# A matmul with RMS norm on one core: block 4's scaled copy in gamma's space, two norms ahead of the evictions, and the head's transposes three matmuls later

## The chip, the cores and the metric

The kernel runs on one core of one Trainium2 chip. The metric is the device time of one execution in microseconds (us). Profile times count from the start of the profiled span, which is 1.8 us shorter than the device time of the same run.

## The reference

```python
def reference(a, b, gamma, eps):          # a, b: 2048 x 2048 float32, gamma: 2048
    x = np.matmul(a, b)
    rms = np.sqrt(np.mean(x ** 2, axis=-1, keepdims=True) + eps)
    return (gamma * x / rms).astype(np.float32)
```

## The kernel before

The output has 16 blocks of 128 rows. Matmuls write into *banks* of the memory called PSUM; copying a finished bank out, by ScalarE or VectorE, is called *evicting* it. A *K tile* is 128 steps of the dimension that is summed over. Blocks 0 to 3 are the "head": while a and b stream in, chunk by chunk, TensorE transposes a's chunk (in a *pair* of K tiles, `kp` = 0 to 7) and multiplies at once. From the right half of blocks 2 and 3 on, and for all later pairs of blocks, the kernel uses Strassen's scheme: seven products ("product 1" to "product 7") of quarter blocks, from sums of quarters that VectorE prepares. Blocks from 4 on are first scaled by a power of two to fp16 (`row_norm`, `row_factor`, `row_apply`), then transposed.

In the code below, `x11` to `x22` are the quarters of one pair's output, `P` is 128, `HB` is 4 (the first block after the head), and left-out lines are marked `...`. Four places matter. First, one PSUM bank, `tbank`, serves both the head's transposes and the one output chunk of the head that finds no bank of its own (`stream_in_parts`):

```python
ps_t = ctx.enter_context(tc.tile_pool(name="ps_t", bufs=1, space=bass.MemoryType.PSUM))

def transpose_head(kp):
    bank = ps_t.tile([P, CH], FP32, name="tbank")
    ...                                            # 8 transposes of 128x128 into it
    nc.vector.tensor_copy(out=head_at[:, 2 * kp:2 * kp + 2, :, :], in_=view)

def stream_in_parts(g, kp):
    part = ps_t.tile([P, CH], FP32, name="tbank")
    ...                                            # 2 matmuls into it, then a copy or an add

for kp in range(KP):
    ...
    before = [lambda: transpose_head(kp + 1)] if kp + 1 < KP else []
    ...
    # the pair's 14 matmuls, with the next pair's transposes after the 7th (12th in pair 0)
    stream(groups1, kp, before, len(groups1) + 5 if kp == 0 else None)
    ...
    stream_in_parts(last1, kp)
    ...
```

Second, block 4's scaled copy goes to the third quarter of `head_at`, which product 3 of the head's Strassen pair still reads:

```python
def a16_slot(mb):
    flat = head_at.rearrange("p t r m -> p (t r m)").bitcast(FP16)
    return flat[:, (2 + mb % 2) * K:(3 + mb % 2) * K]
```

Third, what happens between the head and the first later group; the order of these lines is the order on each engine:

```python
nc.gpsimd.dma_start(out=gamma_sb, in_=gamma.partition_broadcast(P))
load_block(HB + 2)                                  # block 6
load_block(HB + 3)                                  # block 7
...
nc.scalar.copy(out=x22, in_=pair[2])
nc.vector.tensor_tensor(out=x22, in0=pair[5], in1=x22, op=ALU.add)
evict(plain, (2, 3))                                # four banks: two ScalarE, two VectorE
b_sums_in_place(1, KP - 1)
product(PAIR, 1, 4, pair[2], start=False)
row_norm(HB)                                        # ScalarE, block 4
row_norm(HB + 1)                                    # ScalarE, block 5
nc.vector.tensor_tensor(out=x22, in0=pair[1], in1=x22, op=ALU.subtract)
row_factor(HB)                                      # VectorE, four small ones
product(PAIR, 1, 3, pair[5], start=False)
row_apply(HB)                                       # VectorE, 128x2048
nc.scalar.copy(out=x21, in_=pair[2])
row_factor(HB + 1)
row_apply(HB + 1)
...
product(PAIR, 1, 7, p7, within={5: [lambda: turn(HB, 0)]})   # transposes of block 4
turn(HB, 1)
...                                                 # ScalarE copies them out, x12 too
product(PAIR, 1, 6, p6)
a_sums(G0, (5,))
...                                                 # transposes of block 5, VectorE copies
take_rms(0)
a_sums(G0, (2, 1))                                  # the sums for products 2 and 1
```

Fourth, gamma's left half is first read when the left half of block 0 is scaled, some microseconds later.

Of the kernel before, what the change touches and what calls it, by code (L numbers as in the profile page):

```python
# [10 lines left out]
FP16 = mybir.dt.float16  # L11
I32 = mybir.dt.int32
ACTF = mybir.ActivationFunctionType
ALU = mybir.AluOpType
# [3 lines left out]
def kernel(  # L18
# [13 lines left out]
    nc = tc.nc  # L32
    P = 128
# [8 lines left out]
    HALF = N // 2  # L42
    HB = 4
# [34 lines left out]
    spare = [spare[:, 0:CH], consts.tile([P, CH], FP32, name="t_first")]  # L78

    def a16_slot(mb):  # L80
        flat = head_at.rearrange("p t r m -> p (t r m)").bitcast(FP16)
        return flat[:, (2 + mb % 2) * K:(3 + mb % 2) * K]

# [6 lines left out]
    for h, queue in enumerate((nc.sync, nc.scalar)):  # L90
        queue.dma_start(out=a0f[:, 2 * h:2 * h + 2, :],
                        in_=a[2 * h * P:(2 * h + 2) * P, 0:W2].rearrange("(r p) k -> p r k", p=P))
# [10 lines left out]
    def load_head(kp):  # L103
        nc.gpsimd.dma_start(  # L104
            out=ah(kp),
            in_=a[0:HB * P, kp * W2:(kp + 1) * W2].rearrange("(r p) k -> p r k", p=P))
        load_b(0, kp)
# [9 lines left out]
    def load_block(mb):  # L117
        a32[mb] = a_pool.tile([P, K], FP32, name="a32")
        nc.gpsimd.dma_start(out=a32[mb], in_=a[mb * P:(mb + 1) * P, :])
# [27 lines left out]
    gamma_sb = consts.tile([P, N], FP32, name="gamma_sb")  # L147
# [13 lines left out]
    def transpose_head(kp):  # L161
        bank = ps_t.tile([P, CH], FP32, name="tbank")
        view = bank.bitcast(BF16).rearrange("p (t r m) -> p t r m", t=2, r=HB)
        for t in range(2):
            for r in range(HB):
                nc.tensor.matmul(  # L166
                    view[:, t, r, :], ah(kp)[:, r, t * P:(t + 1) * P], identity,
                    is_transpose=True,
                    start=(t == 0 and r == 0), stop=(t == 1 and r == HB - 1),
                )  # L170
        nc.vector.tensor_copy(out=head_at[:, 2 * kp:2 * kp + 2, :, :], in_=view)
# [27 lines left out]
    def new_msq(mb):  # L199
        msq[mb] = msq_pool.tile([P, NCH + 1], FP32, name="msq")  # L200
        n_sq[mb] = 0
# [10 lines left out]
    def row_norm(mb):  # L212

        n2 = stat_pool.tile([P, 2], FP32, name="n2")
        for h in range(2):
            junk = sq_pool.tile([P, 2 * CH], BF16, name="sq")
            nc.scalar.activation(out=junk, in_=a32[mb][:, h * HALF:(h + 1) * HALF],  # L217
                                 func=ACTF.Square, scale=2.0 ** -8, accum_out=n2[:, h:h + 1])
        norm[mb] = stat_pool.tile([P, 1], FP32, name="norm")
        nc.scalar.activation(out=norm[mb], in_=n2[:, 0:1], func=ACTF.Sqrt, bias=n2[:, 1:2],  # L220
                             scale=1.0)

    def row_factor(mb):
        s = stat_pool.tile([P, 1], FP32, name="s")
        nc.vector.tensor_scalar_max(out=s, in0=norm.pop(mb), scalar1=1e-18)
        nc.vector.reciprocal(out=s, in_=s)
        nc.vector.tensor_single_scalar(out=s.bitcast(I32), in_=s.bitcast(I32),  # L227
                                       scalar=0x7F800000, op=ALU.bitwise_and)
        new_msq(mb)
        nc.vector.tensor_scalar(out=msq[mb][:, NCH:], in0=s, scalar1=s, scalar2=float(eps),  # L230
                                op0=ALU.mult, op1=ALU.mult)
        factor[mb] = s

    def row_apply(mb):
        a16[mb] = a16_slot(mb)
        if mb < HB + 2:

            nc.vector.tensor_scalar_mul(out=a16[mb], in0=a32.pop(mb), scalar1=factor.pop(mb))  # L238
        else:
            nc.scalar.activation(out=a16[mb], in_=a32.pop(mb), func=ACTF.Copy,  # L240
                                 scale=factor.pop(mb))


    def quarter(g, r, c):
        if g < G0:
            return head_at[:, c::2, 2 * g + r, :]
        return at(2 * g + r)[:, c::2, :]

    def sum_of(g, s):
        return s_sum[s].bitcast(BF16) if g < G0 else s_sum[s]  # L250

    def a_sums(g, which, lo=0, hi=KP):
        a11, a12, a21, a22 = (quarter(g, r, c) for r in range(2) for c in range(2))
        terms = {1: (a11, a22, ALU.add), 2: (a21, a22, ALU.add), 5: (a11, a12, ALU.add),
                 6: (a21, a11, ALU.subtract), 7: (a12, a22, ALU.subtract)}
        for s in which:
            x, y, op = terms[s]
            nc.vector.tensor_tensor(out=sum_of(g, s)[:, lo:hi, :], in0=x[:, lo:hi, :],  # L258
                                    in1=y[:, lo:hi, :], op=op)
# [4 lines left out]
    def b_sums(j, kp):  # L264

        b11, b12, b21, b22 = (b_quarter(j, kp, r, c) for r in range(2) for c in range(2))
        for n, (x, y, op) in enumerate(((b11, b22, ALU.add), (b12, b22, ALU.subtract),
                                        (b21, b11, ALU.subtract))):
            nc.vector.tensor_tensor(out=sums[j][:, n, kp, :], in0=x, in1=y, op=op)  # L269
# [55 lines left out]
    def x_chunk(mb, c):  # L325
        return x_tile(mb, c // 2)[:, (c % 2) * CH:(c % 2 + 1) * CH]
# [50 lines left out]
    def head_matmul(bank, r, c, kt):  # L377
        nc.tensor.matmul(bank, head_at[:, kt, r, :], head_rhs(c, kt),  # L378
                         start=(kt == 0), stop=(kt == KT - 1))

    def new_bank():
        return ps_a.tile([P, CH], FP32, name="acc")
# [3 lines left out]
    def load_later(n):  # L386
        for _ in range(min(n, len(later))):
            kind, which = later.pop(0)
            load_b(1, which) if kind == "b" else load_half(HB + which // 2, which % 2)

    def stream(groups, kp, before=(), when=None):


        order = [(g, kt) for kt in (2 * kp, 2 * kp + 1) for g in groups]
        if kp == KP - 1 or (kp == 0 and not before):
            order.sort(key=lambda x: groups.index(x[0]))
        for n, (g, kt) in enumerate(order):
            if n == (when or len(groups)):
                for work in before:
                    work()  # L400
            if kt == 0:
                banks[g] = new_bank()
            head_matmul(banks[g], *g, kt)
# [13 lines left out]
    def evict(groups, on_vector):  # L417
        for n, g in enumerate(groups):
            copy = nc.vector.tensor_copy if n in on_vector else nc.scalar.copy
            copy(out=x_chunk(*g), in_=banks[g])  # L420

    PAIR = G0 - 1
    groups1 = [(r, c) for r in range(HB) for c in range(2)][:-1]
# [6 lines left out]
    for kp in range(KP):  # L430
        if kp + 4 < KP:
            load_head(kp + 4)
        else:
            load_later(1)
        before = [lambda: transpose_head(kp + 1)] if kp + 1 < KP else []
        if kp in early_sums:
            before.append(lambda: a_sums(PAIR, *early_sums[kp]))
        stream(groups1, kp, before, len(groups1) + 5 if kp == 0 else None)
        if kp == KP - 1:
            evict(groups1, (1, 3, 5))  # L440
        stream_in_parts(last1, kp)
        if kp > 0:
            b_sums(0, kp - 1)
        if 0 < kp < KP - 2:
            b_sums_in_place(0, kp - 1)
# [4 lines left out]
    plain = [(r, c) for r in range(2) for c in (2, 3)]  # L450
    pair = {}
# [28 lines left out]
    for kp in range(KP):  # L480
# [14 lines left out]
            a_sums(PAIR, (5,), 7, KP)  # L495
        if kp in (3, 4):
            a_sums(PAIR, ((7, 6)[kp - 3],))
    nc.gpsimd.dma_start(out=gamma_sb, in_=gamma.partition_broadcast(P))
    load_block(HB + 2)
    load_block(HB + 3)  # L500

    r2, r3 = HB - 2, HB - 1
    for r in range(HB):
# [1 line left out]
    x11, x12, x21, x22 = (x_chunk(r, c) for r in (r2, r3) for c in (2, 3))  # L505
    nc.scalar.copy(out=x22, in_=pair[2])
    nc.vector.tensor_tensor(out=x22, in0=pair[5], in1=x22, op=ALU.add)
    evict(plain, (2, 3))
    b_sums_in_place(1, KP - 1)
    product(PAIR, 1, 4, pair[2], start=False)  # L510
    row_norm(HB)
    row_norm(HB + 1)
    nc.vector.tensor_tensor(out=x22, in0=pair[1], in1=x22, op=ALU.subtract)
    row_factor(HB)
    product(PAIR, 1, 3, pair[5], start=False)
    row_apply(HB)
    nc.scalar.copy(out=x21, in_=pair[2])
    row_factor(HB + 1)
    row_apply(HB + 1)
    p7 = new_bank()  # L520
    turned = {}

    def turn(mb, g):
        turned[mb, g] = transpose_half(mb, g, g == 0)

    product(PAIR, 1, 7, p7, within={5: [lambda: turn(HB, 0)]})
    turn(HB, 1)
    for g in range(2):
        take_transposed(HB, g, turned[HB, g], nc.scalar.copy)
    nc.scalar.copy(out=x12, in_=pair[5])  # L530
    p6 = new_bank()
    product(PAIR, 1, 6, p6)
    a_sums(G0, (5,))
    for g in range(2):
        turn(HB + 1, g)
        take_transposed(HB + 1, g, turned[HB + 1, g], nc.vector.tensor_copy)
# [289 lines left out]
```

## Time and profile before

The kernel before took 222.55 us (median of three, 222.44 to 222.7). The execution that was profiled took 222.79.

| stretch of the profiled run | us |
|---|---|
| start of pair 1 of the head (until then mostly waits for the first chunks) | 11.68 |
| pair 1 to product 4 of the head's Strassen pair | 46.77 |
| product 4 to product 1 of the next group | 12.83 |
| from there to the end | 149.72 |
| span | 221.0 |

The starts are those of matmuls in the timeline of TensorE (PE).

The page's busy times, and its rows of tenths (one digit for each fortieth of the span), for the kernel before:

```profile
PE 210.2 (95%) x1032; PEld 98.1 (44%) x1032; DVE 165.5 (75%) x326; ACT 127.2 (58%) x263; POOL 35.7 (16%) x76
PE   7999999999999999999999999999999999999950
DVE  1218889999989898979695649855794759797690
DMA  7999999999939595947899149945798349044045
```

PE is busy nearly everywhere. The memory system is too, for the first 60 us, and VectorE (DVE) from 16 us on.

The waits of PE, kernel before (engine, line, what it waited for: us in total, times, longest):

```profile
PE acc L145 <- DVE pace L135: 1.5, 1, 1.5
PE tbank L183 <- DVE head_at L238: 0.4, 1, 0.4
PE tbank L409 <- DVE head_at L171: 0.3, 1, 0.3
PE tbank L166 <- DMA early<-in_a_dram: 0.3, 1, 0.3
PE tbank L166 <- DVE t_left L269: 0.2, 1, 0.2
```

L166 is a transpose of the head, L183 one of block 4 or 5, L409 the part in `stream_in_parts`. Apart from the first line, 1.3 us in all (0.40, 0.35, 0.34 and 0.24 in the timeline). The last line names VectorE, but a's chunk, sent at 15.18 and 10.6 us on its way, landed at 25.8, just when that wait ended: both waits of L166 are for chunks of a.

The timeline of PE, kernel before (start, duration, engine, line, operation, output<-inputs, count, idle time before and what ended it):

```profile
13.69 0.62 PE L166 MATMUL tbank<-identity,early 128*128 128x128 bf16 x8 [0.34 <-DMA early<-in_a_dram]
...
25.80 0.62 PE L166 MATMUL tbank<-identity,early 128*128 128x128 bf16 x8 [0.24 <-DVE t_left L269]
...
58.45 3.62 PE L283 MATMUL acc<-early,head_at 128*128 128x512 bf16 x16
...
63.55 0.62 PE L183 MATMUL tbank<-identity_h,head_at 128*128 128x128 f16 x8 [0.40 <-DVE head_at L238]
...
71.28 1.89 PE L283 MATMUL acc<-t_left,s 128*128 128x512 bf16 x8
```

Products 4 and 3 are the 16 matmuls at 58.45; product 1 of the next group starts at 71.28. The three waits are those that the change is after.

ScalarE (ACT) and VectorE before block 4's transposes, timelines of the kernel before:

```profile
57.84 1.08 ACT L420 COPY x<-acc 128x512 f32<-128x512 f32 x2
58.79 1.08 ACT L217 ACTIVATE sq<-a 128x1024 bf16<-128x1024 f32 x1
...
62.21 1.28 DVE L238 TENSOR_SCALAR head_at<-a,s 128x2048 f16<-128x2048 f32 x1
...
66.35 0.69 DVE L258 TENSOR_TENSOR s<-at_even 128x1024 f16<-128x1024 f16 x1 [0.32 <-ACT at_even L190]
```

Two evictions stand ahead of the norm (L217), and the scaled copy (L238) starts at 62.21, 0.3 us after product 3 stops issuing.

The last long piece of the chain that ended last, kernel before:

```profile
67.88 139.98 PE acc L283 x648
```

From 67.88 us on, 648 matmuls follow each other without a gap, at 0.216 us each. What is to be won must be won ahead of that.

### The profile page before, as it was taken

How to read it: one execution, taken by the hardware profiler on the slowest of the kernel's cores; microseconds unless marked ns; L12 is line 12 of the kernel's file. 1: busy time of each engine (PE TensorE's matmuls, PEld its weight loads, DVE VectorE, ACT ScalarE, POOL GpSimd, SP SyncE). 2: the span in 40 equal slices, each digit the busy share in tenths (PEclk: the TensorE clock that was granted, in tenths of full speed). 3: DMA queues.
4: the chain of work that ended last, by engine and by line, in shares of the span. 5: the costliest groups of instructions: out<-in, count | busy, mean ns of one | idle time of the engine just before them, and what ended most of it. 6: DMA issues, size and time to landing. Idle time of an engine off the chain costs nothing.

```text
span 221.0 us, 3043 instructions
## 1 busy us (share of the span) xinstructions
PE 210.2 (95%) x1032; PEld 98.1 (44%) x1032; DVE 165.5 (75%) x326; ACT 127.2 (58%) x263; POOL 35.7 (16%) x76
## 2 busy tenths in 40 slices
PE   7999999999999999999999999999999999999950
PEld 3545445444445444444444444444444444444430
DVE  1218889999989898979695649855794759797690
ACT  2110002920698898688746997299738995334580
POOL 8544343432000002100200002000200000000040
PEclk9999999999999999999999999999999999999995
DMA  7999999999939595947899149945798349044045
GB/s 153 168 203 206 202 206 210 211 208 234 425 113 363 198 296 114 368 174 212 214 303 408 23 88 270 375 202 95 196 288 371 72 89 386 25 190 193 1 191 191
DMA packets 36576, 46.60 MB, mean 211 GB/s; under 512 B 22224, under 2 KB 26320, under 8 KB 35152
## 3 DMA queue, kind: packets, MB, share of 16 engines
q0 software_dynamic: 10464, 23.86, 43.6%
q1 hardware_dynamic: 25680, 22.02, 33.0%
q10 hardware_dynamic: 416, 0.52, 0.7%
q8 instruction: 8, 0.13, 0.2%
q14 instruction: 8, 0.07, 0.1%
HBM read 34.60 MB, written 16.78 MB: 233 GB/s over the span
## 4 chain that ended last, share of the span: by engine, by line
PE 80%; DMA 9%; DVE 5%; POOL 2%; issue 1%; ACT 1%; DVEq 0%; ACTq 0%; POOLq 0%
PE acc L283 67%; PE acc L378 11%; DMA early<-in_a_dram 4%; DMA b<-in_b_dram 4%; POOL b L100 1%; DVE x L704 1%; PE tbank L409 1%; PE tbank L166 1%; POOL early L104 1%; DVE head_at L238 1%; DVE x L707 1%; DVE t_left L269 0%; PE tbank L183 0%; ACT sq L301 0%; PE acc L183 0%
## 5 line engine op out<-in xcount | busy, mean ns | idle before, releaser
L283 PE MATMUL acc<-b,s 128*128 128x512 bf16 x408 | 93.2, 379 | 0.0
L283 PEld LDWEIGHTS <-s 128*128 128x128 f16 (+1 forms) x512 | 49.9, 98 | 59.9 <-DVE s L258 0.4
L378 PE MATMUL acc<-b,head_at 128*128 128x512 bf16 x176 | 43.3, 381 | 0.0
L301 ACT ACTIVATE sq<-x 128x512 bf16<-128x512 f32 x54 | 34.0, 630 | 6.9 <-DVE x L704 3.0
L360 DVE SCALAR_TENSOR_TENSOR x<-x,r,gamma_sb 128x1024 f32<-128x1024 f32 x28 | 34.8, 1282 | 0.7
L217 ACT ACTIVATE sq<-a 128x1024 bf16<-128x1024 f32 x24 | 25.3, 1054 | 2.4 <-DMA a<-in_a_dram 1.9
L378 PEld LDWEIGHTS <-head_at 128*128 128x128 bf16 x176 | 17.0, 99 | 19.3 <-issue 0.7
L240 ACT ACTIVATE head_at<-a,s 128x2048 f16<-128x2048 f32 x10 | 20.0, 1998 | 3.3 <-DVE s L227 3.3
L100 POOL DMA_DIRECT2D b<-in_b_dram x32 | 17.2, 539 | 20.3 <-DMA b<-in_b_dram 14.4
L420 ACT COPY x<-acc 128x512 f32<-128x512 f32 x6 | 3.4, 590 | 25.0 <-PE acc L378 25.0
L283 PEld LDWEIGHTS <-head_at 128*128 128x128 f16 (+1 forms) x112 | 10.9, 98 | 13.2
L283 PE MATMUL acc<-early,head_at 128*128 128x512 bf16 x64 | 14.5, 379 | 0.0
L283 PEld LDWEIGHTS <-at_even 128*128 128x128 f16 x96 | 9.4, 98 | 11.3
L283 PE MATMUL acc<-early,s 128*128 128x512 bf16 x56 | 14.2, 379 | 0.0
L258 DVE TENSOR_TENSOR s<-head_at 128x1024 f16<-128x1024 f16 (+5 forms) x22 | 13.4, 634 | 0.1
L591 DVE TENSOR_TENSOR x<-x,x 128x512 f32<-128x512 f32 x9 | 6.2, 692 | 8.8 <-ACT x L589 8.3
L125 POOL COPY pace<-x 128x1 f32<-128x1 f32 x4 | 1.7, 413 | 66.3 <-DVE x L600 65.1
L573 ACT COPY x<-acc 128x512 f32<-128x512 f32 x9 | 5.2, 573 | 11.5 <-PE acc L283 7.7
L283 PE MATMUL acc<-t_left,s 128*128 128x512 bf16 x48 | 11.3, 379 | 0.0
L274 DVE TENSOR_TENSOR b<-b 128x1024 bf16<-128x1024 bf16 x16 | 10.8, 683 | 0.2
L283 PE MATMUL acc<-t_left,head_at 128*128 128x512 bf16 x48 | 10.9, 379 | 0.0
L283 PE MATMUL acc<-t_left,at_even 128*128 128x512 bf16 x48 | 10.8, 379 | 0.0
(109 smaller groups left out, 223.6 us busy)
## 6 DMA issues: line engine op xcount, KB each, us to landing
out_dram<-x SPq DMA_DIRECT2D x30, 512.0 KB, 3.7
a<-in_a_dram POOLq DMA_DIRECT2D x10, 1024.0 KB, 8.6
b<-in_b_dram POOLq DMA_DIRECT2D x32, 256.0 KB, 9.8
a<-in_a_dram POOLq DMA_DIRECT2D x4, 512.0 KB, 10.0
early<-in_a_dram POOLq DMA_DIRECT2D x7, 256.0 KB, 10.3
gamma_sb<-in_gamma_dram POOLq DMA_DIRECT2D x1, 1024.0 KB, 11.3
out_dram<-a SPq DMA_DIRECT2D x1, 512.0 KB, 3.1
early<-in_a_dram ACTq DMA_DIRECT2D x1, 256.0 KB, 3.5
```

The costliest lines, as they stand in the source:

```text
L100: nc.gpsimd.dma_start(out=raw[j][kp][:, t, :], in_=b[lo:lo + P, j * HALF:(j + 1) * HALF])
L217: nc.scalar.activation(out=junk, in_=a32[mb][:, h * HALF:(h + 1) * HALF], func=ACTF.Square, scale=2.0 ** -8, accum_out=n2[:, h:h + 1])
L240: nc.scalar.activation(out=a16[mb], in_=a32.pop(mb), func=ACTF.Copy, scale=factor.pop(mb))
L258: nc.vector.tensor_tensor(out=sum_of(g, s)[:, lo:hi, :], in0=x[:, lo:hi, :], in1=y[:, lo:hi, :], op=op)
L274: nc.vector.tensor_tensor(out=flat[:, 1:3, :], in0=flat[:, 1:3, :], in1=flat[:, 0::3, :], op=ALU.add)
L283: nc.tensor.matmul(bank, lhsT[:, kp, :], rhs, start=(start and kp == 0), stop=(kp == KP - 1), skip_group_check=not start)
L301: nc.scalar.activation(out=sq[:, 0:CH], in_=src, func=ACTF.Square, scale=inv_sqrt_n, accum_out=msq[mb][:, c:c + 1])
L360: nc.vector.scalar_tensor_tensor(out=x, in0=x, scalar=inverse_of[mb], in1=gamma_sb[:, h * HALF:(h + 1) * HALF], op0=ALU.mult, op1=ALU.mult)
L378: nc.tensor.matmul(bank, head_at[:, kt, r, :], head_rhs(c, kt), start=(kt == 0), stop=(kt == KT - 1))
L420: copy(out=x_chunk(*g), in_=banks[g])
L573: nc.scalar.copy(out=c, in_=one[1])
L591: nc.vector.tensor_tensor(out=t, in0=t, in1=x12, op=ALU.add)
```

## The change

Its intent: take away PE's wait for block 4's copy, by giving the copy a place that nothing else reads and by putting the norms ahead of the evictions; and let a's chunks come later in the head, by asking for their transposes three matmuls later.

```diff
     def a16_slot(mb):
+        if mb == HB:
+            return gamma_sb[:, 0:HALF].bitcast(FP16)
 ...
-        stream(groups1, kp, before, len(groups1) + 5 if kp == 0 else None)
+        stream(groups1, kp, before, len(groups1) + (5 if kp == 0 else 3))
 ...
-    nc.gpsimd.dma_start(out=gamma_sb, in_=gamma.partition_broadcast(P))
+    load_gamma(1)                                   # the right half
     load_block(HB + 2)
-    load_block(HB + 3)
 ...
-    evict(plain, (2, 3))
+    evict(plain[:2], (0, 1))
+    row_norm(HB)
+    row_norm(HB + 1)
+    evict(plain[2:3], ())
+    row_factor(HB)
+    row_apply(HB)
     b_sums_in_place(1, KP - 1)
     product(PAIR, 1, 4, pair[2], start=False)
-    row_norm(HB)
-    row_norm(HB + 1)
-    nc.vector.tensor_tensor(out=x22, in0=pair[1], in1=x22, op=ALU.subtract)
-    row_factor(HB)
     product(PAIR, 1, 3, pair[5], start=False)
-    row_apply(HB)
     nc.scalar.copy(out=x21, in_=pair[2])
     row_factor(HB + 1)
     row_apply(HB + 1)
+    evict(plain[3:], (0,))
 ...
     turn(HB, 1)
+    load_gamma(0)                                   # the left half
+    load_block(HB + 3)
 ...
     a_sums(G0, (5,))
+    nc.vector.tensor_tensor(out=x22, in0=pair[1], in1=x22, op=ALU.subtract)
```

More of the change, by code (lines that the diff above doesn't have):

```diff
@@ L497, with load_gamma @@
             a_sums(PAIR, ((7, 6)[kp - 3],))
-    nc.gpsimd.dma_start(out=gamma_sb, in_=gamma.partition_broadcast(P))
+    def load_gamma(j):
+        half = slice(j * HALF, (j + 1) * HALF)
+        nc.gpsimd.dma_start(out=gamma_sb[:, half], in_=gamma[half].partition_broadcast(P))
+    load_gamma(1)
     load_block(HB + 2)
-    load_block(HB + 3)
     r2, r3 = HB - 2, HB - 1
```

## The prediction

> What bounds the kernel now. The page gives PE 210.2 of 221.0 us busy; the chain of waits is 80% PE, and from 67.88 to 207.86 us it is one unbroken piece of 648 matmuls at 0.216 us each (139.98 us). The waits of PE after its start add up to little: 0.40 us at the first fp16 transpose of block 4 (63.15 to 63.55, for VectorE's scaled copy), 0.35 us for the first head copy, 0.34 us (13.69) and 0.24 us (25.80) before head transposes. So at most about 1 us can be won.
>
> Why block 4 waits. Its scaled copy is written into a quarter of head_at that the product-3 matmuls still read until 61.9; in the timeline VectorE starts it at 62.21 and ends at 63.50. ScalarE evicts two banks (1.08 us) before the norm of block 4 starts at 58.79. In gamma's space the copy has nothing to wait for but the norm. The norm can start near 57.9, its second half when the data lands (48.78 + 10.0 = 58.8); it is ready near 60.3, the factor (0.7 us) and the 1.28 us copy end near 62.3, 0.8 us before PE asks. The 0.40 us goes.
>
> What is added: one VectorE eviction more (0.6 us) and one ScalarE eviction fewer; the x22 subtraction (0.69 us) moves behind block 4's sum, ahead of the sum for product 2 of the next group. Before, that sum (s) ended near 69.45 and the list of waits shows weight loads waiting 0.42 us for it. After: ScalarE's two transposed copies end near 65.7 instead of 66.3; then a sum, the subtraction, two copies, a total, and the sum for product 2: about 69.0. PE without the stall would ask at 69.05 (earlier if the head gains). So about 0.45 us in total passes this point.
>
> Head transposes three matmuls (0.65 us) later: the DMA landings of a's head chunks (13.65, 17.5, 21.35, 25.8, 29.6, 33.4: issue plus landing time) sit within 0.25 us of PE's requests, so both stalls, 0.58 us, go. The copy to head_at (0.69 us) still has about 1.3 us before the next pair. But then b's chunk for the last pair (lands near 35.9, used at 36.2) allows only 0.3 us. That too meets the sum above.
>
> Gamma's left half and block 7. The load waits for the transposes of block 4 (near 64.5), behind block 6, which now goes out near 63.2 (64.40 before). The Trainium skill, "DMA: Bandwidth & Descriptors", section "Anatomy of one DMA — SWDGE (gpsimd) path", fits 2.0 us + bytes/436e3; for 1 MB that is 4.4 us, and block 6 took 5.0 in this trace. By that (an estimate), the 0.5 MB half lands near 70 and is first used near 73.1 (73.52 before). Block 7 goes out near 65.7 (66.58 before) with 0.5 MB more ahead (1.2 us), lands near 73, as before (66.58 + 6.8 = 73.4), and is wanted at 75.3. No new stall expected.
>
> Predicted: 222.55 - 0.45 = 222.1 us, 8 in 10 between 221.5 and 222.6. Faster by over 2%: 0.01; within 2%: 0.97; slower by over 2%: 0.02.
>
> Right if: the wait of PE for the scaled copy is gone; the waits before head transposes are gone or 0.1 us; weight loads of product 2 still wait for s, PE by 0 to 0.4 us; the unbroken piece starts near 67.4 and the span is near 220.5. Wrong if: VectorE waits at the left-half scaling for gamma (a gap near 73), ScalarE for block 7, or PE for banks evicted later or for head copies at the pairs' starts.

## The result, and the profile after

The changed kernel took 222.24 us (median of six, 222.05 to 222.82) against 222.59 us (222.44 to 222.74) for the kernel before. The ratio is 0.9988, with a 95% interval from 0.9975 to 1.0000. A ratio here is the mean time of one kernel's runs over that of the other's of the same rounds, so it is not quite the ratio of the medians.

The gain in time is thus at the edge of the noise. The profiled execution was the slowest of the six (222.82 us), as that of the kernel before was slow for its kind (222.79), so the two spans are alike. Its page and PE waits, changed kernel:

```profile
PE 210.3 (95%) x1032; PEld 98.2 (44%) x1032; DVE 166.6 (75%) x327; ACT 126.7 (57%) x262; POOL 36.2 (16%) x77
```

```profile
PE acc L147 <- DVE pace L137: 1.5, 1, 1.5
PE acc L380 <- DMA b<-in_b_dram: 0.7, 1, 0.7
PE tbank L411 <- DVE head_at L173: 0.4, 1, 0.4
```

The waits at the transposes (now L168 and L185) are gone. A wait for b's first chunk is new, but it stands before anything that the change touches; it comes back below.

The timeline of PE, changed kernel:

```profile
7.46 2.88 PE L380 MATMUL acc<-b,head_at 128*128 128x512 bf16 x12 [0.70 <-DMA b<-in_b_dram]
...
14.44 0.61 PE L168 MATMUL tbank<-identity,early 128*128 128x128 bf16 x8
14.89 1.03 PE L380 MATMUL acc<-b,head_at 128*128 128x512 bf16 x4
15.84 0.59 PE L411 MATMUL tbank<-b,head_at 128*128 128x512 bf16 x2
16.27 2.32 PE L380 MATMUL acc<-b,head_at 128*128 128x512 bf16 x10
...
36.19 3.49 PE L380 MATMUL acc<-b,head_at 128*128 128x512 bf16 x14
...
58.93 3.62 PE L285 MATMUL acc<-early,head_at 128*128 128x512 bf16 x16
...
63.47 0.61 PE L185 MATMUL tbank<-identity_h,gamma_sb 128*128 128x128 f16 x8
...
71.36 1.89 PE L285 MATMUL acc<-t_left,s 128*128 128x512 bf16 x8
```

The transposes of block 4 start 4.54 us after product 4 (5.10 before). But look at 14.89 to 15.84: four matmuls at 0.216 us are 0.86 us, and the next one comes after 0.95. The list of waits doesn't show these 0.08 us (differences are taken here from unrounded sums), because each matmul's record lasts 0.38 us while the next is due after 0.216; an idle time in the list is the loss less about 0.16 us. By the same reckoning the wait of 0.40 us in the kernel before cost 0.56 us (5.10 - 4.54), and those of 0.34 and 0.24 us cost 0.51 and 0.41 us (pairs of 4.41 and 4.31 us, where the others take 3.90).

ScalarE and VectorE, timelines of the changed kernel:

```profile
15.09 0.69 DVE L173 COPY head_at<-tbank 128x1024 bf16<-128x1024 bf16 x1 [3.29 <-PE tbank L168]
...
58.32 1.06 ACT L219 ACTIVATE sq<-a 128x1024 bf16<-128x1024 f32 x1
...
61.72 1.28 DVE L240 TENSOR_SCALAR gamma_sb<-a,s 128x2048 f16<-128x2048 f32 x1
...
66.35 0.69 DVE L260 TENSOR_TENSOR s<-at_even 128x1024 f16<-128x1024 f16 x1 [0.20 <-ACT at_even L192]
66.96 0.68 DVE L543 TENSOR_TENSOR x<-acc,x 128x512 f32<-128x512 f32 x1
```

The norm now starts at once after the copy of x22, the scaled copy ends at 63.00, 0.5 us before PE asks. L543 is the subtraction that now stands in VectorE's way to the sum for product 2.

GpSimd's (POOL) loads, and the first uses of what they bring, timelines of the changed kernel:

```profile
63.89 0.53 POOL L121 DMA_DIRECT2D a<-in_a_dram  x1 [10.11 <-DVE s L227]
65.47 0.53 POOL L503 DMA_DIRECT2D gamma_sb<-in_gamma_dram  x1 [1.05 <-PE acc L185]
66.09 0.53 POOL L121 DMA_DIRECT2D a<-in_a_dram  x1
...
73.43 1.28 DVE L362 SCALAR_TENSOR_TENSOR x<-x,r,gamma_sb 128x1024 f32<-128x1024 f32 x1
...
75.23 1.06 ACT L219 ACTIVATE sq<-a 128x1024 bf16<-128x1024 f32 x1
```

And how long gamma's half and block 7 took from issue to landing (view of the DMA issues in a window of 0.2 us around each issue, last column in us), changed kernel:

```profile
gamma_sb<-in_gamma_dram POOLq DMA_DIRECT2D x1, 512.0 KB, 7.3
a<-in_a_dram POOLq DMA_DIRECT2D x1, 1024.0 KB, 9.1
```

Block 6 took 5.1 us in the same view. So gamma landed near 72.8 and was used at 73.43; block 7 landed near 75.2 and was used at 75.23. Nothing waited, by less than 0.7 and 0.1 us.

The long piece of the chain, changed kernel:

```profile
68.90 0.67 DVE s L260
69.57 0.05 issue
69.62 138.32 PE acc L285 x640
```

It is shorter by the eight matmuls of product 5, and VectorE's sum for product 2 now stands before it: PE waits for that sum.

### The profile page after: what moved, and what is told of

Read it like the earlier page. It is cut to its first block, busy times and chain, and to the rows that moved or that the text cites. A ratio compares the mean times of both kernels' runs of the same rounds, so it can differ in the third digit from the quotient of the medians. Undisturbed runs are those within 1.5% of the kernel's fastest.

```text
span 221.0 us, 3044 instructions
## 1 busy us (share of the span) xinstructions
PE 210.3 (95%) x1032; PEld 98.2 (44%) x1032; DVE 166.6 (75%) x327; ACT 126.7 (57%) x262; POOL 36.2 (16%) x77
## 4 chain that ended last, share of the span: by engine, by line
PE 72%; DMA 14%; ACT 4%; DVE 4%; POOL 2%; issue 1%; DVEq 0%; ACTq 0%; POOLq 0%
PE acc L285 65%; DMA b<-in_b_dram 9%; PE acc L380 7%; DMA early<-in_a_dram 5%; ACT sq L219 2%; POOL b L102 1%; DVE x L714 1%; ACT at_even L192 1%; POOL early L106 1%; DVE s L260 1%; DVE x L717 1%; ACT sq L303 0%; DVE at_even L192 0%; DVE a L714 0%; DVE x L543 0%
## 5 line engine op out<-in xcount | busy, mean ns | idle before, releaser
L422 ACT COPY x<-acc 128x512 f32<-128x512 f32 x5 | 2.9, 581 | 24.9 <-PE acc L380 24.9
L127 POOL COPY pace<-x 128x1 f32<-128x1 f32 x4 | 1.6, 412 | 66.4 <-DVE x L610 65.7
L583 ACT COPY x<-acc 128x512 f32<-128x512 f32 x9 | 5.2, 573 | 12.8 <-DMA out_dram<-x 12.8
L173 DVE COPY head_at<-tbank 128x1024 bf16<-128x1024 bf16 x7 | 4.8, 692 | 8.6 <-PE tbank L168 8.5
```

The costliest lines, as they stand in the source:

```text
L583: nc.scalar.copy(out=c, in_=one[1])
```

## The experiments

The four stretches of every profile that the argument uses (us):

| run | pair 1 starts | pair 1 to product 4 | product 4 to product 1 | rest | span |
|---|---|---|---|---|---|
| before | 11.68 | 46.77 | 12.83 | 149.72 | 221.0 |
| before again (e8) | 14.02 | 45.85 | 12.82 | 149.71 | 222.4 |
| gamma's space alone (e7) | 11.41 | 47.04 | 12.83 | 149.72 | 221.0 |
| head + 3 alone (e2) | 11.92 | 46.32 | 12.84 | 149.72 | 220.8 |
| head + 2 alone (e10) | 11.86 | 47.65 | 12.84 | 149.75 | 222.1 |
| head + 5 alone (e11) | 11.11 | 48.91 | 12.83 | 149.65 | 222.5 |
| block 4 part alone (e3) | 11.78 | 47.01 | 13.19 | 149.72 | 221.7 |
| changed | 12.29 | 46.64 | 12.43 | 149.64 | 221.0 |
| changed again (e1) | 11.56 | 46.43 | 12.71 | 149.70 | 220.4 |
| changed, sum first (e4) | 11.74 | 46.32 | 12.26 | 149.68 | 220.0 |
| e4 and pair 7 reordered (e5) | 12.34 | 46.32 | 12.26 | 149.68 | 220.6 |
| e5 and head + 2 (e9) | 11.30 | 46.81 | 12.33 | 149.66 | 220.1 |
| changed, copy in its old place (e12) | 12.04 | 46.32 | 12.63 | 150.81 | 221.8 |

The rest is the same to 0.1 us in all but the last. The first column, from 11.1 to 14.0 us, is the luck of the first chunks. It is the largest difference between profiles of one kernel (2.3 us between the two profiles of the kernel before), and the reason why a gain of 0.3 us is hard to see in times. It is partly paid back: where pair 1 starts late (e8), no chunk is waited for later. The head as it was before took 45.85 to 47.04 us in four profiles (before, e3, e7, e8), and with the transposes three matmuls later 46.32 to 46.64 in six. So the later place gains only where a chunk would be waited for.

Theory A said: what the change wins ahead of the next group is capped by VectorE's chain to the sum for product 2. Rival B said: the chunks from memory set the pace, and the order on the engines matters little. Theory C came from the traces of the first eight runs: the transposes' later place makes a new wait, for the one PSUM bank, `tbank`, that serves both the head's transposes and the one output chunk of the head that finds no bank of its own (`stream_in_parts`).

### e1: the changed kernel again

No edit.

> The changed kernel once more, to time it closely and to see whether the first wait for b's first chunk (0.70 us in the profile after, none in the one before) belongs to the change or to the run. Theory A (VectorE's chain to the sum of product 2 sets the gain) and rival B (the chunks of b and a from memory set it): both 0.3 to 0.5 us below the kernel before (222.1 to 222.3). If the wait at 6.8 to 7.5 us is of the run, it is away in this profile in about half the cases; if it is of the change, it is here again.

It took 222.32 us (221.76 to 223.55), the kernel before on the same chip 222.74 us; ratio 0.9985 (0.9954 to 1.0016). In this profile pair 1 started at 11.56 us, so the late start of the other profile belongs to that execution. A wait for b at the start is there again (0.54 us, at 8.39), but also in e8, of the kernel before (2.32 us): it isn't the change's. PE reached product 4 at 57.99 us, 0.94 us earlier than in the first profile, but product 1 of the next group only 0.66 us earlier (70.70 against 71.36). The difference was lost here (timeline of PE):

```profile
68.96 1.90 PE L285 MATMUL acc<-b,s 128*128 128x512 bf16 x8 [0.39 <-DVE s L260]
```

This is product 2, waiting for the sum. The earlier PE comes, the more it waits here: that is the cap of theory A.

### e2: the head part alone

```diff
-        stream(groups1, kp, before, len(groups1) + 5 if kp == 0 else None)
+        stream(groups1, kp, before, len(groups1) + (5 if kp == 0 else 3))
```

> The kernel before with the head transposes three matmuls later and nothing else. A and B: the waits before head transposes (0.34 and 0.24 us) go; b's chunk for the last head pair gives back all but about 0.3 us. A: what is left is lost at block 4's copy or at the sum for product 2, so 0 to 0.2 us faster (222.4 to 222.6). B's opposite (head counts in full): 0.5 us faster.

222.57 us against 222.74; ratio 0.9988 (0.9963 to 1.0013). The waits for a's chunks are gone, and the head takes 46.32 us instead of 46.77. But every one of its first six pairs takes 3.98 us, where the undisturbed pairs of the kernel before take 3.90. Theory C starts here: with the later place, the part that shares `tbank` waits for VectorE's copy of the transposes.

### e3: the block 4 part alone

The changed kernel with the line of e2 undone.

> The change without the later head transposes. A: nearly all of the gain, 0.3 to 0.5 us faster than before (222.1 to 222.3), and the wait of PE for the scaled copy is 0. If the head part carried the gain: under 0.1 us faster (222.5).

222.88 us against 222.74; ratio 0.9999 (0.9974 to 1.0024): the expected gain was not seen. With e2, neither part alone shows a gain clear of noise, so the times don't say which part carries the changed kernel's 0.35 us. The profile fell on the slowest of the six executions, and it shows one way to lose it (timeline of ScalarE):

```profile
58.85 1.06 ACT L219 ACTIVATE sq<-a 128x1024 bf16<-128x1024 f32 x1 [0.96 <-DMA a<-in_a_dram]
```

The first half of block 4 took 10.6 us from issue to landing in this execution, against 9.8 to 10.0 in the other profiles where this was read, and landed at 58.8. ScalarE was ready for it from 57.9 on and had to wait; the copy then came 0.34 us too late for PE (4.88 instead of 4.54 us after product 4), and the list of waits has PE waiting another 0.51 us for the sum for product 2. Once the evictions are out of its way, the norm is at the mercy of the memory stream. Whether the other five executions of this kernel had the same is not known, since only one is profiled.

### e4: the changed kernel with the sum for product 2 first

```diff
-    nc.vector.tensor_tensor(out=x22, in0=pair[1], in1=x22, op=ALU.subtract)   # after a_sums(G0, (5,))
 ...
-    take_rms(0)
-    a_sums(G0, (2, 1))
+    a_sums(G0, (2,))
+    take_rms(0)
+    nc.vector.tensor_tensor(out=x22, in0=pair[1], in1=x22, op=ALU.subtract)
+    a_sums(G0, (1,))
```

> The changed kernel with the subtraction of pair 1 (0.69 us on VectorE) moved behind the sum for product 2 and ahead of the sum for product 1, and that sum also ahead of the row total. A: the sum is ready 0.75 us earlier (near 68.8), weight loads no longer wait 0.59 us for it, PE no longer waits 0.17 us or more; 0.2 to 0.4 us below the changed kernel (221.8 to 222.0). B: no change against the changed kernel (within 0.1 us).

222.33 us against 222.32 for e1 on the same chip; ratios 0.9977 (0.9952 to 1.0001) and 0.9985. Theory A's gain of 0.2 to 0.4 us in time was missed, and B's forecast of no change met, but one kernel's executions differ by more than that (221.79 to 222.9), so the times don't decide. The stretch does: product 4 to product 1 takes 12.26 us, 0.17 and 0.45 us less than in the two profiles of the changed kernel. The sum started at 67.83 (68.22 in e1, 68.87 in the first profile; timeline of VectorE):

```profile
67.83 0.69 DVE L260 TENSOR_TENSOR s<-at_even 128x1024 f16<-128x1024 f16 x1
```

The list of PE's waits no longer names it (weight loads still wait 0.4 us for it). Theory A holds for this stretch; e1 and e4 reached product 4 at nearly the same time, 57.99 and 58.06, so memory doesn't explain the difference.

### e5: e4, and the last pair of the head reordered

```diff
             order.sort(key=lambda x: groups.index(x[0]))
+            if kp == KP - 1:
+                order[0:6] = order[0:6:2] + order[1:6:2]
```

> The kernel of the run before, and in the last pair of the head the first three groups take their first-half matmuls before their second-half ones, so that b's last half chunk is asked for two matmuls (0.43 us) later. A and B agree that the wait inside the last head pair (about 0.3 us, between the 1st and 2nd matmul) goes. With the sum out of the way this should pass to the end: 0.2 to 0.3 us below the kernel with only the sum moved (221.5 to 221.8). If another gate follows right after, under 0.1 us.

222.29 us (221.68 to 224.8) against 222.68; ratio 0.9984 (0.9943 to 1.0026), so nothing is shown by the times. In its profile pair 7 took 3.45 us, the shortest seen (3.75 in the first profile of the changed kernel, 3.53 in e1), but it took no longer in e4, which has the old order. The wait inside pair 7 comes and goes with the stream, and this edit was not put to the test here.

### e6: the changed kernel without gamma's space, as first tried

```diff
     def a16_slot(mb):
-        if mb == HB:
-            return gamma_sb[:, 0:HALF].bitcast(FP16)
```

> The changed kernel, but block 4's copy goes to its old place in head_at (gamma's halves are still loaded apart). The copy must then wait for the end of product 3 (about 62.0 to 62.5 us), as before: it ends near 63.7, PE waits 0.3 to 0.6 us at the transposes, and the time is 222.4 to 222.7, as before. If the earlier norm alone made the gain, it stays at 222.2.

Wrong results (relative error 0.49) and 227.05 us. This was a mistake in the experiment: the changed order issues the copy ahead of product 3, which then reads what the copy has overwritten. PE must even wait for the copy before products 4 and 3 (timeline of PE):

```profile
62.56 4.45 PE L283 MATMUL acc<-early,head_at 128*128 128x512 bf16 x12 [3.23 <-DVE head_at L238]
```

It tells what gamma's space is for: only with it may the copy stand ahead of product 3 in the program. It is mended in e12.

### e7: gamma's space alone

The kernel before with the new `a16_slot`, the two loads of gamma with block 7's load behind the second, and nothing else of the change.

> The kernel before with block 4's copy in gamma's space and gamma's left half loaded later, the norms, evictions and subtraction left as they were. In the profile before VectorE starts the factor at 61.51, at once after its other work, and the copy at 62.21, when product 3 is already over (61.9): so the space alone gives nothing (222.5 to 222.7, PE still waits 0.3 to 0.4 us). If the place was the cause, as the prediction put it: 0.3 to 0.4 us faster.

222.73 us against 222.68; ratio 0.9991 (0.9964 to 1.0018). The transposes come 5.09 us after product 4, as before, and product 4 to product 1 takes 12.83 us. The place by itself gives nothing: the copy starts at 62.21 in either place, straight behind VectorE's other work. The norm and VectorE's order held it as long as product 3 did.

### e8: the kernel before again

No edit.

> The kernel before once more, for a second profile of it: times within 0.1 us of 222.55. The wait for b's first chunk at the start differs from profile to profile by some tenths of a us; the waits of 0.34 and 0.24 us before head transposes are then smaller or gone when the start was late, since the chunks come by the clock of the memory, not of PE.

223.09 us against 222.68 for the same kernel beside it, ratio 1.0023 (0.999 to 1.0057): two sets of one kernel differed by 0.4 us in the median, which is the size of the effect under study. In its profile the first chunk of b kept PE for 2.3 us; no chunk was waited for afterwards, and all six pairs took 3.90 us, as expected of a late start.

### e9: e5 with the head's transposes two matmuls later instead of three

```diff
-        stream(groups1, kp, before, len(groups1) + (5 if kp == 0 else 3))
+        stream(groups1, kp, before, len(groups1) + (5 if kp == 0 else 2))
```

> The run with the sum first and the last head pair reordered, and the head transposes two matmuls later than before in place of three. Theory C, from the traces: with three, the part of the last block that shares the transposes' PSUM bank waits 0.08 us in each of six pairs for VectorE's copy of the transposes (a pair takes 3.98 us, 3.91 in the kernel before). With two the pairs take 3.91 us, and the stretch from pair 1 to product 4 takes 45.9 to 46.0 us where no chunk is waited for (46.32 with three). Time 0 to 0.45 us below the run with three (221.6 to 222.2); what the memory stream holds back is not won.

221.9 us (221.74 to 222.33) against 222.89 us; ratio 0.9958 (0.9946 to 0.997). This is the fastest kernel, and the only one whose gain over the kernel before is clear of noise, though still far below 2%. It ran on another chip than the changed kernel, and the two were not timed side by side; nor is it known which of its three additions (sum first, pair 7, two in place of three) makes the gain. Pairs that waited for nothing took 3.90 us, as theory C says. The stretch to product 4 was not shorter than with three (46.81), since this execution started early (11.30) and waited for a's chunks: the stream took back what the bank gave. Even so product 4 came at 58.11 us, 0.3 us after block 4's first half had landed, which suggests (no run shows it) that little is left to win before the stream itself is the limit.

### e10: the head part with two matmuls, alone

The edit of e9 on the kernel before.

> The kernel before with the head transposes two matmuls later and nothing else. C: pairs of 3.91 us, no bank wait, and waits for a's chunks of at most 0.1 us: pair 1 to product 4 in 45.9 to 46.3 us (46.77 before; 46.32 with three). Rival (the pair is long because the copies come late to the next pair, or because of the memory stream): 3.98 us as with three.

222.82 us against 222.89; ratio 1.0003 (0.9988 to 1.0019). From the start of the transposes to the part in their bank took 1.52 to 1.54 us in all six pairs, which is eight transposes (0.45 us) and five matmuls (1.08) without a gap, and the three pairs that waited for no chunk took 3.90 us, not 3.98: no bank wait, which is theory C against its rival. One such pair (timeline of PE):

```profile
21.79 0.61 PE L166 MATMUL tbank<-identity,early 128*128 128x128 bf16 x8
22.23 1.24 PE L378 MATMUL acc<-b,head_at 128*128 128x512 bf16 x5
23.31 0.59 PE L409 MATMUL tbank<-b,head_at 128*128 128x512 bf16 x2
```

The expected length of the stretch was missed: the profiled execution, the slowest of six, waited 1.25 us for one of a's chunks at 27.10 us, and the stretch took 47.65 us.

### e11: the head part with five matmuls, alone

```diff
-        stream(groups1, kp, before, len(groups1) + 5 if kp == 0 else None)
+        stream(groups1, kp, before, len(groups1) + 5)
```

> The kernel before with the head transposes five matmuls later in every pair, so that only two matmuls stand between them and the part in the same bank. C: the bank wait grows by two matmuls (0.43 us) in each of the six pairs: pairs of 4.41 us, 2.6 us more than with three in all, the time 2 to 2.8 us above the kernel before (224.6 to 225.4). Rival (memory stream): pairs stay near 3.98 us, time within 0.3 us of before.

225.11 us against 222.89; ratio 1.0088 (1.0074 to 1.0101). The six pairs took 4.41 us each (one 4.42), as theory C had it to the hundredth. PE's waits in this run:

```profile
PE tbank L409 <- DVE head_at L171: 2.5, 7, 0.4
```

Seven waits of 0.35 us (each costing 0.51) for VectorE's copy, at the matmuls that want the transposes' bank: six in these pairs, and the one in pair 0 that every kernel here has. The rival, that the stream sets the pairs' length, falls. The arithmetic closes too: 3.90 us needs the copy done by the time the bank is asked for; three matmuls exceed that by 0.08, five by 0.08 + 2 x 0.216 = 0.51.

### e12: the changed kernel with the copy in its old place, after product 3

```diff
-        if mb == HB:
-            return gamma_sb[:, 0:HALF].bitcast(FP16)
 ...
     row_factor(HB)
-    row_apply(HB)
     b_sums_in_place(1, KP - 1)
     product(PAIR, 1, 4, pair[2], start=False)
     product(PAIR, 1, 3, pair[5], start=False)
+    row_apply(HB)
```

> The changed kernel with block 4's copy back in head_at, this time issued after product 3 that reads there (the earlier try put it ahead and was wrong). The copy waits for the end of product 3, 3.6 us after product 4 starts, and ends 4.9 us after; the transposes come near 5.0 (4.54 in the changed kernel, 5.10 in the one before). Product 4 to product 1 of the next group: 12.8 to 13.2 us (12.43 and 12.71 in the two profiles of the changed kernel, 12.83 before). If the earlier norm alone made the gain: 12.4 to 12.7 us.

223.55 us against 222.89; ratio 1.0033 (1.0018 to 1.0047): slower than the kernel before. The transposes came 4.83 us after product 4, less late than expected, and the stretch took 12.63 us, which is within what the rival ("the earlier norm alone") expected. So in this stretch the earlier norm and factor carry half of the gain (5.10 to 4.83), and the copy's place in gamma's space and in VectorE's order the other half (4.83 to 4.54). These two are not separated: behind product 3 the copy also stands behind an in-place sum of b on VectorE (61.25, 0.68 us), and it started at 61.85, straight after that sum, with no wait for product 3 to be seen. But the rest of the kernel took 1.1 us longer, which nobody expected. It begins with block 6's load (timelines of POOL and ScalarE in this run):

```profile
64.05 1.15 POOL L119 DMA_DIRECT2D a<-in_a_dram  x1 [10.64 <-ACT x L521]
...
71.31 1.06 ACT L217 ACTIVATE sq<-a 128x1024 bf16<-128x1024 f32 x1 [1.44 <-DMA a<-in_a_dram]
```

The load must wait for the copy, because it overwrites what the copy reads. But that is not the cause: it went out 5.69 us after product 4 here and 5.95 us after it in the kernel before, whose rest is not longer. It took 7.2 us to land, though (5.0 in the kernel before, 5.1 in the changed kernel). ScalarE waited 1.44 us for it, VectorE 2.06 us for the norm, and PE 0.31 and 0.46 us (as the timeline lists them) for VectorE's work behind that. Gamma's half and block 7 were sent 1.1 and 1.7 us behind the load, but in e7, with 1.15 and 2.17 us, it landed after 5.1. Why it took 2 us longer here, and why POOL took 1.15 us to issue it instead of 0.53, stays open.

## Why the prediction was right, and where it was not

- **The time.** Predicted 222.1 us, 221.5 to 222.6; measured 222.24. Predicted gain 0.45 us; 0.35 by the medians. The range was wide enough to hold the kernel before too (222.59), so the time alone tests little. That the size fits is in part luck: the stalls to be removed were 1.48 us and not the 0.98 of the list, and a wait that was not foreseen took 0.48 back. By stretches, from pair 1 to product 1 of the next group, the account closes: 1.48 - 0.48 (bank) - 0.30 (b's chunk) - 0.17 (sum) = 0.53 us in the first profile, measured 59.60 - 59.07.
- **PE's wait for block 4's copy goes.** Right in the changed kernel; its size was misread. The idle of 0.40 us in the list was a loss of 0.56 us, since matmuls' records overlap their successors. The prediction gave the place in `head_at` as the cause. In the kernel before that was not what held the copy: the place alone gives nothing (e7), the earlier norm and factor alone 0.27 us (e12), all together 0.56.
- **The gain is capped by the sum for product 2.** Right: PE lost 0.17 and 0.45 us there against e4, which takes VectorE's subtraction out of the way. Against the whole, 12.83 us became 12.43 and 12.71, instead of the 12.26 that were to be had.
- **The head: "both stalls, 0.58 us, go".** They went, and they had cost more, 0.92 us. What failed is the step "The copy to head_at (0.69 us) still has about 1.3 us before the next pair". It asked the wrong question. The first to want the copy done is not the next pair but the part that shares the bank, 0.86 us after the transposes stop issuing; that is 0.08 us too soon, in each of six pairs: 0.48 us. The list of waits had shown it in pair 0, as the wait of L409 for L171. The prediction put that down as a wait for the first head copy, without asking why this matmul, which reads nothing of that copy, needs it: for the bank.
- **b's chunk for the last pair.** Right in kind: pair 7 took 3.75 and 3.53 us in two profiles of the changed kernel, against 3.45, so 0.30 and 0.08 us were held back.
- **Gamma's half near 70, block 7 near 73.** Wrong by 2.8 and 2.2 us in the first profile (72.8 and 75.2), without consequence, because uses came at 73.43 and 75.23. Part of it is the issue: gamma's half went out at 65.47 instead of near 64.5, block 7 at 66.09 instead of near 65.7. The other 1.8 us of each lie between issue and landing. The Trainium skill, "DMA: Bandwidth & Descriptors", section "Anatomy of one DMA — SWDGE (gpsimd) path", gives 2.0 us + bytes/436e3 for one DMA. The prediction reckoned with the loads ahead at the rate in that fit (an estimate: 1.2 us for 0.5 MB). Block 6, with no other load of its queue ahead of it, took 5.1 us for 1 MB (4.4 by the fit). Gamma's half landed 3.8 us after it and not 1.2; block 7 landed 2.4 us after that, which is the fit's rate for 1 MB. So the step that failed is the 1.2 us for gamma's half. From 69 to 70 us, 65 of 67 packets were under 8 KB and the DMA engines moved 274 GB/s; from 67 to 68 us none was, and they moved 410 GB/s. Whether the smaller packets, the loads beside it or the one row of gamma that is read for every partition slow it, no run here separates.
- **The long piece starts near 67.4.** The prediction contradicted itself here: with PE waiting at the sum, the chain's piece starts behind that wait, at 69.62 in the first profile and 68.96 in e1. The span, predicted near 220.5, was 221.0 in the first profile and 220.4 in e1.

Still open: what the change is worth in time (neither 0.9988 nor e1's 0.9985 is clear of noise); why the block 4 part alone showed no gain in time (e3); why pair 1 starts anywhere between 11.1 and 14.0 us; and how far e9 is ahead of the changed kernel on one chip.

## What to carry to other kernels

When an instruction is moved later, look for every reader of what it produces and every next user of the buffer it fills; in a rotating bank the next user often comes first, and a small regular gap in each round is its sign. The Trainium skill, "Perfetto Trace Analysis", section "Optimization Strategy", says that the same gap repeating on the engine that should be saturated can mean too few buffers in SBUF or PSUM; here it was one bank for two uses, 0.08 us a round, too short for the list of waits to show. When one execution's luck is larger than the gain, cut the profile into stretches whose starts don't depend on that luck, and compare those.

## What the Trainium skill lacked or had wrong

- "DMA: Bandwidth & Descriptors": the fit of 2.0 us + bytes/436e3 is for one transfer; how long loads of one queue take when they are sent one behind another is not given as a figure. Here 0.5 MB behind 1 MB took 7.3 us and landed 3.8 us after it, where its bytes at the fit's rate are 1.2 us (an estimate); 1 MB behind both took 9.1 us. The chunks of the head, 256 KB each as written, with many outstanding, mostly took about 10 us each.
- "Perfetto Trace Analysis", section "Optimization Strategy": it tells the reader to find the gaps between slices, but does not say how much of a gap the overlap of matmul records hides. Here records of 0.38 us at a spacing of 0.216 us hide about 0.16 us of each gap: 0.40 us shown was 0.56 lost, and gaps of 0.08 us were not shown at all. (A latency and a spacing of matmuls do stand on another page, "TensorE: Matmul & The Clock Gate"; no page that was read carries them over to the gaps of a trace.)
- No page that was read gives the spread of the first loads of a kernel. Here the head's second pair started between 11.1 and 14.0 us in 13 profiles, with the same instructions up to that point.
